# The blockwise recurrence of a decoder layer: 16x16 inverses by halves, two DMA queues, new issue times

## The chip, the cores and the metric

The kernel runs on one core of one Trainium2 chip, as one launch. The metric is the device time of an execution in microseconds; the median of several runs is compared. The engines are TensorE (PE: matrix products and transposes), VectorE (DVE), ScalarE (ACT), GpSimd (Pool) and SyncE (SP, which here only issues transfers).

## The reference

One layer of a decoder on 256 tokens of width 1024, float32. Two token mixers run side by side on the normalised input and come from one combined input projection: an RWKV-7 recurrence of 8 heads of 64, and softmax attention of 8 heads of 64. Both are projected, gated, summed and projected again; a gated MLP with a width-3 convolution follows. The part that matters here is the recurrence, one state of 64x64 for each head:

```python
def step(state, inp):
    r_t, w_t, k_t, v_t, a_t, b_t = inp           # a_t = -kk, b_t = kk * a
    sa = jnp.einsum('bhvk,bhk->bhv', state, a_t)
    state = (state * w_t[:, :, None, :] + sa[..., None] * b_t[:, :, None, :]
             + v_t[..., None] * k_t[:, :, None, :])
    return state, jnp.einsum('bhvk,bhk->bhv', state, r_t)
...
x = x + (g_a * u_a + g_b * u_b) @ w_out[l]
x = x + conv_ffn(rms_norm(x, norm2_g[l]), w_ffn_up[l], ffn_conv_w[l], ffn_conv_b[l], w_ffn_down[l])
```

## The kernel before, in words

All large products are done with a number split in two parts. Weights arrive from memory as `raw` tiles of 512 KB, loaded by SP into 4 buffers. ACT rounds each to a high half (`whi`, L259), DVE subtracts to get the low half (`wlo`, L269, 3 buffers), and PE uses both. One weight tile feeds two bulk blocks of PE, each of 12 matmuls with 256 columns (L302, L304, L307) or 6 with 512 columns (L323, L324, L327).

The recurrence is computed in 4 chunks of 64 tokens for 8 heads. Within a chunk it needs the inverse of a unit triangular 64x64 matrix for each of 32 pairs of head and chunk. In order of the program:

- `KB` (L645, L647) are keys scaled by the decay, one product of them on Pool; `AR` (L651) holds the other factors. PE turns KB (`pk`, L670; ACT copies to `KBt`, L673).
- PE multiplies KB and AR into `pgr` (L682) in two halves of 32 matmuls; DVE masks them into `G` (L686). Both halves use the same four PSUM banks.
- The diagonal 16x16 blocks of G go out to memory (`d1`, L707) and back as `Tb` (L709), one block on each of 128 partitions. DVE inverts them row by row, 15 steps of a product and a sum (L717, L719), copies the transpose (L720), and SP writes both forms, `Xb`, to memory (`d2`, L722). 24 transfers bring them back into `X` (L729), 16 on SP and 8 on Pool. X[:, 0] holds the inverse, X[:, 1] its transpose.
- PE turns the values (`pv`, L748) and multiplies them by G (`pz`, L760). Then come the bonus and gate products (`ch`, `pg`, L841 to L846), which take one weight tile of their own; Pool casts a part of it (L833) for L846.
- PE joins the 16-blocks to 32 and then 64: `pp` (L791, reads X[:, 0]), DVE masks it to `P` (L797), `px` (L808, L818, read X[:, 1]), DVE adds into X (L801, L824, L827), and once more.
- Four chunk steps follow (L933 to L973), each with a group normalisation (L892 to L903, with one operation on Pool, L900), whose result PE turns (`pc`, L910).

The order of PE's work is written out by hand. The recurrence (`chain`), the attention (`att`), the normalisation (`gn`) and the bulk projections (`bulk`) are generators. Each yields a cost and a latency; a planner keeps a clock, adds the cost to it, and calls a generator again once the clock has passed the time of its last yield plus its latency. The bulk generator has latency 0 and fills what is left. A bulk block costs 0.33 x 4 or 0.65 x 2. A number `yield 0, 11.0` is thus an issue time: bulk work of 11 in the plan is put ahead of what follows. PE executes in the order of issue. On the other engines and queues the framework's scheduler sets the order. `taken` counts the weight tiles, and `GATE_AT` is the place of the gate tile in the queue of loads; the assertion at L831 ties it to the plan.

After the generators come the second branch projection, the output projection and the MLP, which the change does not touch.

Of the kernel before, what the change touches and what calls it, by code (L numbers as in the profile page):

```python
# [9 lines left out]
F32 = mybir.dt.float32  # L10
# [3 lines left out]
OP = mybir.AluOpType  # L14
AX = mybir.AxisListType
# [13 lines left out]
HALF = 8  # L29
NORM_EPS = 1e-6  # L30
GN_EPS = 64e-5
GATE_AT = 30
SLACK = {"chain": 1.7, "att": 1.4, "lv1": 2.5, "gn": 2.0}
DEC = math.exp(-0.5)
NEG = -3.0e38
# [2 lines left out]
def body(tc, x, positions, norm1_g, w_in, rwkv_mu, w_decay_up, decay_bias, w_aaa_up,  # L38
         aaa_bias, w_gate_up, k_k, k_a, r_k, ln_g, ln_b, q_norm_g, k_norm_g, w_branch_a,
         w_branch_b, w_out, norm2_g, w_up, conv_w, conv_b, w_down, out):  # L40
    nc = tc.nc
    act, dve, pool, pe = nc.scalar, nc.vector, nc.gpsimd, nc.tensor
    ctx = ExitStack()
    with ctx:
# [22 lines left out]
        def b2(name, shape, dt=F32):  # L67
            return sb.tile(shape, dt, name=name, tag="b2", bufs=9)
# [95 lines left out]
            return par[:, i:i + 1]  # L164

        wdu = cst.tile([128, CW], F32, name="wdu")
        cst.tile([128, 848], F32, name="gap")
        gqk = cst.tile([128, 2, 64], F32, name="gqk")
        posi = sb.tile([128, 2], I32, name="posi")

# [1 line left out]
        for r, n in ((mu1[0:1792].rearrange("(n c) -> n c", c=128), 14),  # L172
# [3 lines left out]
            dst = p1[at_:at_ + n]  # L176
# [341 lines left out]
        def ch16(t):  # L518
            return t.rearrange("p a (c i) -> p (a c) i", i=64)
# [31 lines left out]
        def need(nm, d):  # L551
            while nm not in d:
                yield 0, 0.5
# [6 lines left out]
        def chain():  # L560
# [71 lines left out]
            def kbv(q, a):  # L632
                return KB[:, 64 * q:64 * q + 2048].rearrange("p (u a i) -> p u a i", a=2, i=64)[:, :, a]
# [8 lines left out]
            bb = av  # L642
            dve.tensor_tensor(flat(bb), flat(kk), flat(av), op=OP.mult)
            yield 0, 1.0
            pool.tensor_tensor(kbv(0, 1), ch16(bb), ch16(e3), op=OP.mult)  # L645
            for q, hs in PAR:
                dve.tensor_tensor(kbv(q, q)[hs], ch16(kp)[hs], ch16(e3)[hs], op=OP.mult)  # L647
                yield 0, 1.0
# [7 lines left out]
            G = [b8(f"G{q}", [128, 16, 128]) for q in range(2)]  # L656
            d1 = dr.tile([128, 256], F32, name="d1")
            d2 = dr.tile([8, 2, 16, 256], F32, name="d2")
            Tb = sb.tile([128, 16, 16], F32, name="Tb")
            def banks(nm):  # L660
                return [[(chp if j else atp)(nm) for _ in range(2)] for j in range(2)]

            yield 0, 4.0

            KBt = [b2("KBt", [128, 4, 128]) for _ in range(3)]
            pk = [[p.rearrange("p (c a i) -> p c a i", c=2, a=4) for p in pj] for pj in banks("pk")]
# [4 lines left out]
            for c in range(3):  # L671
                for q, hs in PAR:
                    act.copy(KBt[c][:, :, hs], pk[c // 2][q][:, c % 2])  # L673
            yield 1.4, 4.0
            masks()
            for g in range(2):
                pg = [[p.rearrange("p (u i) -> p u i", u=4) for p in pj] for pj in banks("pgr")]
                for ct in (2 * g, 2 * g + 1):
                    for c in range(4):
                        u = 4 * ct + c  # L680
                        for q, hs in PAR:
                            pe.matmul(pg[ct % 2][q][:, c], kb(q, u), AR[hs, u].rearrange("p a i -> p (a i)"),  # L682
                                      start=True, stop=True)
                for ct in (2 * g, 2 * g + 1):
                    for q in range(2):
                        last_g = dve.tensor_tensor(G[q][:, gslot(ct):gslot(ct) + 4], pg[ct % 2][q],  # L686
                                                   gmask[:, None, :].to_broadcast([128, 4, 128]), op=OP.mult).ins
                yield 2.1, (5.0, 0.1)[g]
            bp = zr
            bph, bpl = by("bph", dt=F32R), by("bpl", dt=F32R)  # L690
            xgh, xgl = b2("xgh", [128, 2, S], F32R), t1("xgl", dt=F32R)
# [11 lines left out]
            for q, hs in PAR:  # L703
                for b in range(4):
                    q0 = bsl(q).start + 16 * b
                    r0 = (q * 4 + b) * 16
                    nc.sync.dma_start(d1[r0:r0 + 16].rearrange("u (j i) -> j u i", j=16),  # L707
                                      G[q][q0:q0 + 16, :, 16 * b:16 * b + 16])
                nc.sync.dma_start(Tb[hs], d1[hs].rearrange("u (j i) -> u j i", j=16))  # L709
            Xb = b2("Xb", [128, 2, 16, 16])  # L710
            dve.memset(Xb[:, 0], 0.0)
            dve.memset(Xb[:, 0].rearrange("p i n -> p (i n)")[:, 0:256:17], 1.0)
            tmp = sb.tile([128, 64], F32, name="tmp")
            for j in range(15):
                ni, nn = 15 - j, j + 1
                tv = tmp[:, :ni * nn].rearrange("p (i n) -> p i n", i=ni)
                dve.tensor_tensor(tv, Tb[:, j, j + 1:16][:, :, None].to_broadcast([128, ni, nn]),  # L717
                                  Xb[:, 0, j, 0:nn][:, None, :].to_broadcast([128, ni, nn]), op=OP.mult)
                dve.tensor_tensor(Xb[:, 0, j + 1:16, 0:nn], Xb[:, 0, j + 1:16, 0:nn], tv, op=OP.add)  # L719
            dve.tensor_copy(Xb[:, 1], Xb[:, 0].rearrange("p i n -> p n i"))  # L720
            for xx in range(2):
                nc.sync.dma_start(d2[:, xx], Xb[:, xx].rearrange("p i n -> p (i n)"))  # L722
            X = b8("X", [128, 2, 16, 64])
            pool.memset(X, 0.0)

            def to_x(eng, side, x, us_, src):
                b = src[1]
                q0 = bsl(side).start + 16 * b
                eng.dma_start(X[q0:q0 + 16, x, us_, 16 * b:16 * b + 16],  # L729
                              d2[4 * src[0] + b, x, src[2]].rearrange("u (i n) -> i u n", i=16))  # L730

            for q in range(2):
                for b in range(4):
                    to_x(nc.sync, q, 0, slice(0, 16), (q, b, slice(0, 16)))
            for q in range(2):
                for b in range(4):
                    for a in range(2):
# [1 line left out]


            yield from need("v", zs)
            zv = zs["v"]
            VU = b8("VU", [128, 4, 2, 4, 64])
            pv = [chp("pv").rearrange("p (j a n) -> p j a n", j=2, a=4) for _ in range(2)]
# [81 lines left out]
                    v = level(1, w, X[bsl(a), 1, 8 * q + 1:8 * q + 8:2])  # L826
                    dve.tensor_tensor(v, v, p[1][bsl(1 - a), 0:4], op=OP.add)  # L827

            yield 0, 11.0
            yield 0, 2.0  # L830
            assert taken[0] == GATE_AT, taken[0]  # L831
            wgh, wgl = weights()
            pool.tensor_copy(wgh[64:128, 1], wgl[64:128, 1].bitcast(F32))  # L833
# [542 lines left out]
```

## Time and profile before

| | us |
|---|---|
| median of 3 runs | 405.56 |
| lowest and highest | 405.13, 407.06 |
| span of the profiled execution, first to last instruction | 403.9 |
| PE busy | 396.4 |
| DVE busy | 324.6 |
| ACT busy | 233.9 |
| Pool busy | 41.8 |

The page tells of one profiled execution. It gives the span from its first to its last instruction, and not that execution's own device time; the three runs lie 1.2 to 3.2 above the span. "Idle before" is the time in which an engine did nothing, with the instruction or transfer whose end let it go on. A wait that ended with "issue" has no releaser in the profile. A line of the timeline has the start, the duration, the engine, the line of the program, the operation and out<-in; "x" counts the instructions merged. Times in the text are in us from the start of the span.

### The profile page before, as it was taken

The numbers are of one execution on the slowest core, as the hardware profiler recorded it, in microseconds if no ns is written. First come the engines' busy times: TensorE is split into PE (matmuls) and PEld (weight loads), VectorE is DVE, ScalarE is ACT, GpSimd is POOL, SyncE is SP. The second block draws the span as 40 slices with busy tenths as digits, with TensorE's granted clock in tenths as the row PEclk, the third lists the DMA queues.
The fourth block names the chain that finished last, engine by engine and source line by source line (L and its number), as shares of the span: only waits on it lengthen the run. The fifth ranks groups of instructions, "written<-read, shape, count | busy, mean of one in ns | idle before, by whom it ended". The sixth has DMA issues, their size and how long they took to land.

```text
span 403.9 us, 8280 instructions
## 1 busy us (share of the span) xinstructions
PE 396.4 (98%) x3250; PEld 348.7 (86%) x3250; DVE 324.6 (80%) x574; ACT 233.9 (58%) x397; POOL 41.8 (10%) x69
## 2 busy tenths in 40 slices
PE   7999999999989999999999999999999999999996
PEld 3999989788989989999888888888888888888885
DVE  3988999899667978778965898977869778687694
ACT  6799755475647676444563784655546446355440
POOL 7910070010500011020011000000000000000000
PEclk9999999999999999999999999999999999999999
DMA  8954555564783444536563756676665665656612
GB/s 243 317 168 154 160 161 158 160 176 150 159 220 104 115 150 131 183 112 207 191 183 97 242 157 208 181 232 189 200 204 163 208 187 177 207 174 209 196 48 104
DMA packets 61990, 70.53 MB, mean 175 GB/s; under 512 B 9421, under 2 KB 52243, under 8 KB 61952
## 3 DMA queue, kind: packets, MB, share of 16 engines
q1 hardware_dynamic: 61104, 69.54, 57.1%
q0 software_dynamic: 832, 0.47, 0.6%
q8 instruction: 25, 0.41, 0.5%
q14 instruction: 13, 0.11, 0.1%
q10 hardware_dynamic: 16, 0.00, 0.0%
HBM read 68.56 MB, written 1.44 MB: 173 GB/s over the span
## 4 chain that ended last, share of the span: by engine, by line
PE 93%; DVE 2%; ACT 1%; DMA 1%; issue 1%; SPq 0%; POOL 0%; DVEq 0%; POOLq 0%; ACTq 0%
PE acc L1262 15%; PE acc L302 9%; PE acc L304 8%; PE acc L307 8%; PE acc L1267 8%; PE at L1262 5%; PE acc L323 5%; PE acc L327 5%; PE acc L324 5%; PE f L1286 5%; PE f L1282 5%; PE f L1284 4%; PE at L1267 3%; PE acc L461 1%; DMA x<-in_x_dram 1%; PE pgr L682 1%
## 5 line engine op out<-in xcount | busy, mean ns | idle before, releaser
L259 ACT CAST whi<-raw 128x1024 fp32r<-128x1024 f32 x120 | 125.7, 1051 | 106.0 <-PE acc L1262 22.2
L269 DVE TENSOR_TENSOR wlo<-raw,whi 128x1024 fp32r<-128x1024 f32 x121 | 148.8, 1234 | 26.2 <-PE acc L1267 12.2
L1262 PE MATMUL acc<-hx,whi 128*128 128x512 f32 x264 | 68.2, 393 | 0.0
L302 PE MATMUL acc<-hx,whi 128*128 128x256 f32 x232 | 58.3, 287 | 0.0
L304 PE MATMUL acc<-hx,whi 128*128 128x256 f32 x232 | 55.9, 277 | 0.0
L1262 PEld LDWEIGHTS acc<-hx,whi 128*128 128x128 f32 x264 | 47.0, 188 | 8.1
L302 PEld LDWEIGHTS acc<-hx,whi 128*128 128x128 f32 x232 | 43.6, 188 | 2.0 <-issue 0.8
L304 PEld LDWEIGHTS acc<-hx,whi 128*128 128x128 f32 x232 | 43.6, 188 | 0.1
L1267 PEld LDWEIGHTS acc<-h,wlo 128*128 128x128 f32 x264 | 37.1, 188 | 3.6
L1267 PE MATMUL acc<-h,wlo 128*128 128x256 f32 x264 | 37.8, 279 | 0.0
L307 PE MATMUL acc<-hx,wlo 128*128 128x256 f32 x232 | 35.7, 277 | 0.0
L1284 PE MATMUL f<-whi,hb 128*128 128x512 f32 x80 | 31.2, 390 | 0.0
L1286 PE MATMUL f<-wlo,hb 128*128 128x512 f32 x80 | 31.2, 390 | 0.0
L1282 PE MATMUL f<-whi,hb 128*128 128x512 f32 x80 | 31.2, 389 | 0.0
L307 PEld LDWEIGHTS acc<-hx,wlo 128*128 128x128 f32 x232 | 30.6, 188 | 0.0
L1262 PE MATMUL at<-hx,whi 128*128 128x512 f32 x88 | 24.0, 392 | 0.0
L1272 DVE TENSOR_REDUCE an<-acc 128x256 f32<-128x512 f32 x22 | 14.2, 685 | 9.3 <-PE acc L1267 9.3
L1262 PEld LDWEIGHTS at<-hx,whi 128*128 128x128 f32 x88 | 16.4, 188 | 3.6
L323 PE MATMUL acc<-whi,hx 128*128 128x512 f32 x48 | 19.1, 399 | 0.0
L324 PE MATMUL acc<-whi,hx 128*128 128x512 f32 x48 | 18.8, 391 | 0.0
L1286 PEld LDWEIGHTS f<-wlo,hb 128*128 128x128 f32 x80 | 15.0, 188 | 3.2
L1284 PEld LDWEIGHTS f<-whi,hb 128*128 128x128 f32 x80 | 15.0, 188 | 2.8
(331 smaller groups left out, 688.5 us busy)
## 6 DMA issues: line engine op xcount, KB each, us to landing
raw<-in_w_ffn_up_dram SPq DMA_DIRECT2D x44, 512.0 KB, 4.3
raw<-in_w_in_dram SPq DMA_DIRECT2D x37, 512.0 KB, 4.3
raw<-in_w_ffn_down_dram SPq DMA_DIRECT2D x22, 512.0 KB, 4.0
raw<-in_w_out_dram SPq DMA_DIRECT2D x8, 512.0 KB, 4.1
x<-in_x_dram SPq DMA_DIRECT2D x8, 256.0 KB, 4.4
early<-in_w_in_dram SPq DMA_DIRECT2D x4, 512.0 KB, 7.6
raw<-in_w_branch_b_dram SPq DMA_DIRECT2D x4, 512.0 KB, 3.4
raw<-in_w_branch_a_dram SPq DMA_DIRECT2D x4, 512.0 KB, 3.5
```

The costliest lines, as they stand in the source:

```text
L259: act.copy(wide(hi, k, c), spread(raw, k, c))
L269: eng.tensor_tensor(wide(lo, k, c), spread(raw, k, c), wide(hi, k, c).bitcast(F32), op=OP.subtract)
L302: pe.matmul(om, wh[:, k, ms], xh[:, k0 + k], start=k0 + k + m == 0, stop=False, skip_group_check=True)
L304: pe.matmul(om, wh[:, k, ms], xl[:, k0 + k], start=False, stop=False, skip_group_check=True)
L307: pe.matmul(om, wl[:, k, ms], xh[:, k0 + k], start=False, stop=k0 + k == nk - 1 and m == n - 1, skip_group_check=True)
L323: pe.matmul(ps_[t], xh[:, K, ts], wh[:, k], start=K == 0, stop=False)
L324: pe.matmul(ps_[t], xl[:, K, ts], wh[:, k], start=False, stop=False)
L1262: pe.matmul(ps_[m], wh[:, k, m * 128:m * 128 + 128], hx[:, k0 + k].rearrange("p a s -> p (a s)"), start=k0 + k == 0, stop=False, skip_grou ...
L1267: pe.matmul(ps_[m][:, 0:S], wl[:, k, m * 128:m * 128 + 128], h2[k0 // 4][:, k], start=False, stop=k0 + k == 7, skip_group_check=True)
L1282: pe.matmul(fin[f], hb[:, 0, i, ts], wh[:, 0, cs], start=st, stop=False, skip_group_check=f == 3)
L1284: pe.matmul(fin[f], hb[:, 1, i, ts], wh[:, 0, cs], start=False, stop=False, skip_group_check=f == 3)
L1286: pe.matmul(fin[f], hb[:, 0, i, ts], wl[:, 0, cs], start=False, stop=False, skip_group_check=f == 3)
```

## The change

Five edits, all in the recurrence:

1. The Pool product of KB (L645) goes to DVE.
2. The 16x16 blocks are inverted by halves: the four 4x4 blocks on the diagonal row by row (4 small operations), then 4 to 8 and 8 to 16, each as two products with `product`: all terms into `tmp`, then a reduction. Tb is read back in the order in which it was written, one contiguous row for each partition, and DVE transposes while it copies into Xb. The two memsets of Xb become one of the diagonal. Tb and Xb are 272 wide, so that the diagonal blocks can be addressed with one stride.
3. The transfers of d1, Tb, d2 and the first 8 of X alternate between SP and Pool, by side. The queues then have 4 + 1 + 1 + 12 each, where SP had 8 + 2 + 2 + 16 and Pool 8.
4. Issue times: ahead of pk 4.0 becomes 2.0, behind pk 4.0 becomes 3.5, between the two pgr 5.0 becomes 3.0, ahead of pv 1.5 is new, and ahead of the gate products 11.0 + 2.0 becomes 6.0. GATE_AT follows, 30 to 27.
5. Places in memory: `gap`, a tile that nothing uses, shrinks from 848 to 336 columns, `tmp` moves to the shared buffers `b2`, Xb gets a place of its own, and `wv` is new.

```diff
-GATE_AT = 30
+GATE_AT = 27
...
-        cst.tile([128, 848], F32, name="gap")
+        cst.tile([128, 336], F32, name="gap")
...
-            pool.tensor_tensor(kbv(0, 1), ch16(bb), ch16(e3), op=OP.mult)
+            dve.tensor_tensor(kbv(0, 1), ch16(bb), ch16(e3), op=OP.mult)
...
-            Tb = sb.tile([128, 16, 16], F32, name="Tb")
+            Tb = sb.tile([128, 272], F32, name="Tb")
...
-            yield 0, 4.0
+            yield 0, 2.0
...
-            yield 1.4, 4.0
+            yield 1.4, 3.5
...
-                yield 2.1, (5.0, 0.1)[g]
+                yield 2.1, (3.0, 0.1)[g]
...
-                    nc.sync.dma_start(d1[r0:r0 + 16].rearrange("u (j i) -> j u i", j=16),
-                                      G[q][q0:q0 + 16, :, 16 * b:16 * b + 16])
-                nc.sync.dma_start(Tb[hs], d1[hs].rearrange("u (j i) -> u j i", j=16))
-            Xb = b2("Xb", [128, 2, 16, 16])
-            dve.memset(Xb[:, 0], 0.0)
-            dve.memset(Xb[:, 0].rearrange("p i n -> p (i n)")[:, 0:256:17], 1.0)
-            tmp = sb.tile([128, 64], F32, name="tmp")
-            for j in range(15):
-                ni, nn = 15 - j, j + 1
-                tv = tmp[:, :ni * nn].rearrange("p (i n) -> p i n", i=ni)
-                dve.tensor_tensor(tv, Tb[:, j, j + 1:16][:, :, None].to_broadcast([128, ni, nn]),
-                                  Xb[:, 0, j, 0:nn][:, None, :].to_broadcast([128, ni, nn]), op=OP.mult)
-                dve.tensor_tensor(Xb[:, 0, j + 1:16, 0:nn], Xb[:, 0, j + 1:16, 0:nn], tv, op=OP.add)
-            dve.tensor_copy(Xb[:, 1], Xb[:, 0].rearrange("p i n -> p n i"))
+                    (nc.sync, nc.gpsimd)[q].dma_start(d1[r0:r0 + 16].rearrange("u (j i) -> j u i", j=16),
+                                                      G[q][q0:q0 + 16, :, 16 * b:16 * b + 16])
+                (nc.sync, nc.gpsimd)[q].dma_start(Tb[hs, 0:256], d1[hs])
+            Xb = sb.tile([128, 2, 272], F32, name="Xb")
+            tmp = b2("tmp", [128, 512])
...
+            X0 = Xb[:, 0]
+            dve.tensor_copy(X0[:, 0:256].rearrange("p (i n) -> p i n", n=16),
+                            Tb[:, 0:256].rearrange("p (j i) -> p i j", i=16))
+            dve.memset(X0[:, 0:256:17], 1.0)
+            td, xd = diagonal(Tb), diagonal(X0)
+            for j in (1, 2):
+                ni = 3 - j
+                tv = tmp[:, 0:4 * ni * j].rearrange("p (b i n) -> p b i n", b=4, i=ni)
+                dve.tensor_tensor(tv, td[:, :, j, j + 1:4][:, :, :, None].to_broadcast([128, 4, ni, j]),
+                                  xd[:, :, j, 0:j][:, :, None, :].to_broadcast([128, 4, ni, j]), op=OP.mult)
+                dve.tensor_tensor(xd[:, :, j + 1:4, 0:j], xd[:, :, j + 1:4, 0:j], tv, op=OP.add)
...
+            def product(dst, x, y, n):
+                tv = tmp[:, 0:n * n * n].rearrange("p (i m k) -> p i m k", i=n, m=n)
+                dve.tensor_tensor(tv, x[:, :, None, :].to_broadcast([128, n, n, n]),
+                                  y.rearrange("p k m -> p m k")[:, None, :, :].to_broadcast([128, n, n, n]),
+                                  op=OP.mult)
+                dve.tensor_reduce(dst, tv, axis=AX.X, op=OP.add)
+            for n in (4, 8):
+                for o in range(0, 16, 2 * n):
+                    w = wv[:, 0:n * n].rearrange("p (i m) -> p i m", i=n)
+                    product(w, square(Tb, o, o + n, n).rearrange("p k i -> p i k"), square(X0, o, o, n), n)
+                    product(square(X0, o + n, o, n), square(X0, o + n, o + n, n), w, n)
+            dve.tensor_copy(Xb[:, 1, 0:256].rearrange("p (n i) -> p n i", n=16),
+                            X0[:, 0:256].rearrange("p (i n) -> p n i", i=16))
             for xx in range(2):
-                nc.sync.dma_start(d2[:, xx], Xb[:, xx].rearrange("p i n -> p (i n)"))
+                (nc.sync, nc.gpsimd)[xx].dma_start(d2[:, xx], Xb[:, xx, 0:256])
...
-                    to_x(nc.sync, q, 0, slice(0, 16), (q, b, slice(0, 16)))
+                    to_x((nc.sync, nc.gpsimd)[q], q, 0, slice(0, 16), (q, b, slice(0, 16)))
...
             yield from need("v", zs)
+            yield 0, 1.5
...
-            yield 0, 11.0
-            yield 0, 2.0
+            yield 0, 6.0
```

More of the change, by code (lines that the diff above doesn't have):

```diff
@@ new lines, in chain, with square, diagonal @@
+                (nc.sync, nc.gpsimd)[q].dma_start(Tb[hs, 0:256], d1[hs])
+            Xb = sb.tile([128, 2, 272], F32, name="Xb")
+            tmp = b2("tmp", [128, 512])
+            def square(t, r0, c0, n):
+                return t[:, 16 * r0 + c0:16 * r0 + c0 + 16 * n].rearrange("p (i n) -> p i n", n=16)[:, :, 0:n]
+            def diagonal(t):
+                return t[:, 0:272].rearrange("p (b r) -> p b r", r=68)[:, :, 0:64].rearrange(
+                    "p b (i n) -> p b i n", n=16)[:, :, :, 0:4]
@@ new lines, in chain @@
+            wv = sb.tile([128, 64], F32, name="wv")
+            def product(dst, x, y, n):
[9 more added lines that the diff above has]
+                    product(square(X0, o + n, o, n), square(X0, o + n, o + n, n), w, n)
```

## The prediction

> **What bounds the kernel now.** I read the page's head first, then who TensorE (PE) waits for, then the busy time by stage, and only then the rows of the changed stage.
>
> ```profile
> span 403.9 us, 8280 instructions
> PE 396.4 (98%) x3250; PEld 348.7 (86%) x3250; DVE 324.6 (80%) x574; ACT 233.9 (58%) x397; POOL 41.8 (10%) x69
> ```
>
> The list of PE's waits (who waited for whom: us in total, times, longest):
>
> ```profile
> PE idle L109 <- DVE eps L374: 1.5, 1, 1.5
> PE px L808 <- issue: 1.1, 1, 1.1
> PE pc L910 <- DVE yc L903: 0.6, 1, 0.6
> PE xt L414 <- DVE xn L408: 0.6, 1, 0.6
> ```
>
> Busy time by stage (stretch, its length, then PE, PEld, DVE, ACT, POOL, granted clock, DMA share, GB/s):
>
> ```profile
> 14.00:60.00 46.00, 46.00 (x407) 42.90 (x406) 42.68 (x68) 35.48 (x58) 14.65 (x24) 1.00 0.61 184
> 60.00:110.00 50.00, 50.00 (x453) 44.30 (x453) 44.26 (x108) 30.42 (x50) 6.53 (x11) 1.00 0.60 162
> 110.00:184.00 74.00, 72.22 (x1152) 67.20 (x1151) 57.74 (x118) 43.74 (x103) 6.48 (x9) 1.00 0.50 146
> ```
>
> PE is busy in 98% of the span. The list of PE's waits is complete: two belong to the start, which the change does not touch, and two to the recurrence, 1.1 and 0.6. The stretches 14 to 60 and 60 to 110, where the vector engine (DVE) runs at 93% and 89%, cost PE nothing: it is busy for 46.00 of 46.00 and 50.00 of 50.00. The granted clock is 1.00 throughout. The change removes no matmul, so what it can win is about the 1.7 us of recurrence waits; what it can lose has no such ceiling.
>
> **The change part by part.** PE runs in the order in which the planner hands out work, so shorter issue times only reorder PE. A bulk block costs 1.32 or 1.30 in the plan (0.33 x 4, 0.65 x 2) and 1.36 on PE, the distance of the first two rows here; the second fence has the recurrence's stages (start us, us, then the instruction).
>
> ```profile
> 64.20 0.28 PE L302 MATMUL acc<-hx,whi 128*128 128x256 f32 x1
> 65.56 0.28 PE L302 MATMUL acc<-hx,whi 128*128 128x256 f32 x1
> ```
>
> ```profile
> 60.48 0.97 PE L670 MATMUL pk<-ident,KB 64*128 64x64 f32 x24
> 67.02 2.06 PE L682 MATMUL pgr<-AR,KB 64*128 64x128 f32 x32
> 74.70 2.06 PE L682 MATMUL pgr<-AR,KB 64*128 64x128 f32 x32
> 84.62 1.16 PE L760 MATMUL pz<-VU,G 64*64 64x64 f32 x64
> 105.60 0.28 PE L846 MATMUL pg<-xgh,whi 128*128 128x256 f32 x1
> 114.93 1.14 PE L791 MATMUL pp<-X,G 64*64 64x32 f32 x64
> 118.83 0.82 PE L808 MATMUL px<-P,X 64*64 64x32 f32 x41
> 120.70 0.49 PE L808 MATMUL px<-P,X 64*64 64x32 f32 x20 [1.05 <-issue]
> 146.94 0.41 PE L910 MATMUL pc<-ident,yc 128*128 128x128 f32 x2 [0.63 <-DVE yc L903]
> ```
>
> Stepping the planner through both sets of yields gives the bulk blocks between stages. Between the key product and pk there are 2 fewer blocks; between pk and the first pgr 3 instead of 4 (3.5 / 1.32 rounds up to 3, 4.0 to 4), between the two pgr 3 instead of 4, between the second pgr and pz 8 instead of 5 (the new 1.5 and where it falls), and from pz to the gate product 8 instead of 14. So pk moves to 60.48 - 2 x 1.36 = 57.8, pgr to 62.9 and 69.3, pz to 83.3, the first L846 to 105.60 - 7 x 1.37 = 96.0. That is three weight tiles less, which agrees with GATE_AT 27 for 30. Then pp comes at 105.4 and px at 109.5: the attention's two transposes of 0.65 that stood before pp now come behind it, and 5 blocks stand where 4 stood. No block is added or lost. What remains is whether each input is there.
>
> Pool's product. These rows price it:
>
> ```profile
> 51.26 1.22 DVE L643 TENSOR_TENSOR av<-sq,av 128x1024 f32<-128x1024 f32 x1
> 56.49 2.74 DVE L269 TENSOR_TENSOR wlo<-raw,whi 128x1024 fp32r<-128x1024 f32 x1
> 52.65 5.50 POOL L645 TENSOR_TENSOR KB<-av,L 128x1024 f32<-128x1024 f32 x1 [30.96 <-DVE av L643]
> ```
>
> It takes 5.50 us on Pool and ends at 58.15; the same shape takes DVE 1.22, so KB would be ready at about 53.7, 4 us ahead of pk at 57.8. On Pool it would be 0.35 late. DVE gains 1.22 of work in a stretch where it is 93% busy. Against that, one weight split (L269) took 2.74 during the Pool product where its like takes 1.22: 1.52 may come back. Net DVE cost between -0.3 and +1.2; I take 0 for PE, because PE never waited for a split in this stretch. [...]
>
> The earlier G. pgr's second half needs the banks that the first half's mask products free. The nearest rows are DVE's:
>
> ```profile
> 68.78 2.47 DVE L686 TENSOR_TENSOR G<-pgr,gmask 128x512 f32<-128x512 f32 x4
> ```
>
> and, for the inversion, the groups of DVE between 60 and 110 (count, busy us, mean ns):
>
> ```profile
> L719 DVE TENSOR_TENSOR Xb<-Xb,tmp 128x15 f32<-128x15 f32 (+7 forms) x15 | 3.1, 204 | 0.3
> L717 DVE TENSOR_TENSOR tmp<-Tb,Xb 128x15 f32<-128x15 f32 (+7 forms) x15 | 3.0, 202 | 0.3
> L994 DVE TENSOR_REDUCE r<-s 128x8 f32<-128x512 f32 x2 | 1.3, 659 | 0.4 <-ACT s L992 0.4
> L848 DVE TENSOR_TENSOR zr<-ch,zv 128x512 f32<-128x512 f32 x1 | 0.7, 684 | 0.0
> L720 DVE COPY Xb<-Xb 128x256 f32<-128x256 f32 x1 | 0.4, 390 | 0.0
> ```
>
> pgr's first half would end at 64.9. If DVE takes the mask products then, the first two banks are free by 66.2 and PE at 69.3 waits for nothing; if they start no earlier than now, at 68.78, plus 1.22 of added work, the first two end at 71.2 and PE waits 2.0. I take 0.3, near the low end, because the splits that stood ahead of these products belong to tiles that PE now needs later.
>
> The inversion. Before: 3.0 + 3.1 + 0.4 and two memsets of 0.35 together, about 6.9 us in 33 dependent instructions. After: two copies at 0.39, a memset under 0.1, four small products at 0.16, four products and four reductions of 64 at 0.203 (the mean of the old steps, which have 15 to 64 elements), two products of 512 at 0.684 and two reductions of 512 at 0.659: 0.78 + 0.07 + 0.64 + 1.62 + 1.37 + 1.32 = 5.8 us in 19 instructions. The reductions of 64 have no row; between 0.16 and 0.66 each the total lies between 5.6 and 7.6. This saves PE nothing by itself: nobody on PE waits for it.
>
> The transfers, by the rows of SP and Pool, and then the times to landing (in order: G to memory, Tb, X from SP, X from Pool):
>
> ```profile
> 85.31 0.46 SPq L709 DMA_DIRECT2D Tb<-d  x1
> 101.88 1.39 SPq L722 DMA_DIRECT2D d<-Xb  x2
> 105.22 7.62 SPq L729 DMA_DIRECT2D X<-d  x16
> 112.95 6.69 SPq L236 DMA_DIRECT2D raw<-in_w_in_dram  x5
> 103.55 1.47 POOL L833 CAST whi<-wlo 64x512 fp32r<-64x512 f32 x1 [15.41 <-DVE wlo L269]
> 107.01 4.30 POOL L729 DMA_DIRECT2D X<-d  x8 [1.98 <-DMA d<-Xb]
> ```
>
> ```profile
> DMA to landing us min/median/max: 1.6/1.7/2.0
> DMA to landing us min/median/max: 4.6/4.6/4.6
> DMA to landing us min/median/max: 1.8/1.9/2.7
> DMA to landing us min/median/max: 1.9/2.1/2.4
> ```
>
> One issue costs about 0.47 on SP and 0.53 on Pool. With G ready at 72.7 (1.7 behind the second pgr's end, as now), four issues, 1.7 to land, one Tb issue and 2 to 4.6 to land, Tb is there at 79 to 81.5. It was issued at 85.31 and took 4.6 in the queue with weight loads; Pool's half avoids that queue. The inversion then ends at 87 to 92, Xb lands 2 to 3 later, and each queue issues 12 transfers of X (SP 5.6 us, Pool 6.4): the last X lands between 98 and 103.5. pp needs its half at 105.4, px the rest at 109.5, so both are covered by at least 2 us. If Tb comes later than DVE's order expects, the weight splits behind the inversion wait with it; three wlo buffers of 2.7 us of PE each are the cover.
>
> [...] The unused tile "gap" shrinks by 512 columns to make room for the wider Xb; I price it at 0, since no row ties time to placement.
>
> The two waits. The 1.05 at px stands between instructions of one kind and waits for nothing that the profile shows. It falls where five 512 KB loads, held back behind SP's 16 X issues until 112.95, are in flight. After the change SP is held 5.6 rather than 7.6 us, and px comes at 109.5, about 9 behind the end of SP's X issues rather than 6. Bounds: it goes (-1.05), or stays or moves elsewhere (0), or appears twice (+1.05). I take -1.05, because the queue ahead of it drains earlier. [...] At pc the group normalisation has 6.5 us of other PE work ahead of it instead of 6.1, so 0.63 becomes about 0.3; bounds 0 and 1.2.
>
> Sum: -1.05 - 0.3 + 0.3 = -1.05 us, so a span of 402.8. The profiled execution's time outside its span is not on the page; the median of the runs, 405.56, stands 1.7 above the span, and I carry that over: 404.5.
>
> **The rivals.**
> (1) Nothing moves: the pause at px is bound to the density of small matmuls and comes back, pc as before: 405.6. For it: the same 96 small matmuls follow each other in px. Against it: the other dense stages, pp and pgr, show no such pause.
> (2) Slower, by Pool's queue. L833 casts half of the gate weights on Pool, takes 1.47 and ended at 105.02, 0.6 before the first L846. It now has to end by 96.0. If the 12 X issues (from 91, when Xb has landed, for 6.4 us) stand ahead of it in Pool's order, it ends at 91 + 6.4 + 1.5 = 98.9 and PE waits 2.9 at L846, with all bulk work behind it: 405.56 - 1.05 + 2.9 = 407.4, up to 409 if Xb lands 2 later. It decides as soon as Xb lands before the gate tile's low half is split. Now Xb landed at 107.0, behind the cast; by my working the two come within 2 us of each other.
> (3) All recurrence waits go and nothing new comes: 405.56 - 1.7 = 403.9. A busy PE is not PE at its peak, so the true waits can be longer than listed; I allow 0.7 for that, down to 403.2.
> (4) The vector engine holds pgr back by 2.0: 405.56 - 1.35 + 2.0 = 406.2.
>
> **How the numbers follow.** Chances: forecast 0.45 (its own range 403.6 to 405.2), rival 1 0.18, rival 2 0.20, rival 3 0.12, rival 4 0.05. Half a per cent, 2.0 us, is about what a measurement of this kernel can tell from no change. Faster than 403.5 takes rival 3 and the edge of the forecast: 0.15. Slower than 407.6 takes the upper half of rival 2 and what I have not thought of: 0.18. Same: 0.67. The range takes in all cases but the tails, with 0.2 below rival 3 for the spread of the runs: 403.0 to 408.2.
>
> **What would show it.** Right: KB written by DVE before 55, pk near 57.8, pgr near 62.9 and 69.3, the gate product near 95.4, the last X landed before 104, a list of PE's waits without px. Rival 2: PE's wait at pg L846 with Pool as releaser. Rival 4: a wait at pgr L682. Wrong altogether: a wait of PE for weight splits (L269) around the inversion, a Tb that lands after 84, or a PE busy time that differs by more than the waits.

## The result and the profile after

The changed kernel takes 411.67 us (median of 6 runs, 411.05 to 413.25); the kernel before took 406.33 beside it. The ratio is 1.0121, with a 95% interval of [1.0091, 1.0152]: slower by 1.2%, where 404.5 was forecast. The profiled execution of the changed kernel took 413.25, the longest of its runs, with a span of 411.2.

The head of the page of the changed kernel, the list of PE's waits (in total, times, longest) and the busy time by stage follow, in the order in which the prediction shows them of the kernel before:

```profile
span 411.2 us, 8270 instructions
PE 399.6 (97%) x3250; PEld 350.0 (85%) x3250; DVE 328.0 (80%) x561; ACT 233.2 (57%) x397; POOL 42.7 (10%) x78
```

```profile
PE xt L414 <- DVE xn L408: 1.5, 1, 1.5
PE idle L109 <- DVE eps L374: 1.5, 1, 1.5
PE acc L323 <- DVE qkv L1027: 1.2, 1, 1.2
PE pS L986 <- DVE yf L945: 0.8, 1, 0.8
PE pc L940 <- DVE yc L933: 0.7, 1, 0.7
PE acc L327 <- DVE wlo L269: 0.6, 1, 0.6
PE acc L302 <- ACT whi L259: 0.6, 1, 0.6
PE pv L779 <- DVE zv L491: 0.5, 1, 0.5
PE acc L461 <- DVE hx L422: 0.4, 1, 0.4
```

```profile
14.00:60.00 46.00, 45.37 (x388) 41.67 (x389) 42.30 (x66) 35.33 (x56) 11.08 (x22) 1.00 0.54 163
60.00:110.00 50.00, 47.64 (x421) 41.45 (x421) 46.40 (x100) 27.34 (x48) 12.63 (x23) 1.00 0.59 162
110.00:184.00 74.00, 72.44 (x1154) 66.77 (x1153) 55.08 (x112) 44.04 (x105) 5.17 (x6) 1.00 0.49 145
```

Two waits on the list belong to the start (L414, L461) and are longer here than in the execution shown of before; in the profiles of the variants below they come and go (first row of the table), so that part is the profiled execution's. The pause at px is gone. Five waits are new: L302 in the stretch 14 to 60, pv, L327 and L323 between 60 and 110, and pS (L986) in the chunk steps. All but L302 have the vector engine as releaser. The stretch 60 to 110, in which PE had been busy for 50.00 of 50.00, now has 47.64.

The listed waits understate it. I therefore took, for every matmul, the distance to the next start beyond the median distance for its shape in the kernel before, and summed that by stage. A stage begins with the first matmul that it names; pss (L603) is the norm of the keys. The table has the differences to the kernel before, in us, each from the one profiled execution; its columns are the changed kernel and six variants that the experiments introduce. The sums agree with the differences of the spans within 0.3:

| stage | after | memset_held | place_only | after_old_times | times_only | inv_later | late_t12 |
|---|---|---|---|---|---|---|---|
| first 14 us | +1.3 | +0.3 | 0.0 | -0.4 | -0.6 | +0.3 | -0.4 |
| 14 to pss (L603) | +1.8 | -0.1 | 0.0 | +1.4 | +0.1 | 0.0 | -0.1 |
| pss to pv | +0.1 | 0.0 | 0.0 | +0.1 | +0.6 | +0.2 | 0.0 |
| pv to the gate product | +3.1 | +3.1 | +2.2 | +6.9 | +1.5 | +0.6 | +0.9 |
| gate product to pp | 0.0 | 0.0 | 0.0 | +0.1 | +3.1 | +1.1 | -0.1 |
| pp to the last pc | +0.3 | +0.3 | -0.2 | -1.6 | +2.9 | +9.4 | +1.7 |
| behind it | +0.6 | +0.6 | 0.0 | 0.0 | +0.6 | +0.6 | -0.3 |
| sum | +7.2 | +4.2 | +2.0 | +6.6 | +8.2 | +12.2 | +1.8 |

Apart from the start, the loss of the changed kernel thus has two main places, 14 to pss and pv to the gate product. The experiments ask why.

### The profile page after: what moved, and what is told of

Its sections match the earlier page's. It is cut to its first block, busy times and chain, and to the rows that moved or that the text cites. A ratio compares the mean times of both kernels' runs of the same rounds, so it can differ in the third digit from the quotient of the medians.

```text
span 411.2 us, 8270 instructions
## 1 busy us (share of the span) xinstructions
PE 399.6 (97%) x3250; PEld 350.0 (85%) x3250; DVE 328.0 (80%) x561; ACT 233.2 (57%) x397; POOL 42.7 (10%) x78
## 4 chain that ended last, share of the span: by engine, by line
PE 77%; DVE 12%; ACT 4%; issue 2%; DMA 2%; POOL 2%; SPq 0%; DVEq 0%; POOLq 0%; ACTq 0%
PE acc L1292 15%; PE acc L1297 7%; PE acc L302 6%; PE acc L307 5%; PE acc L304 5%; PE at L1292 5%; PE f L1314 4%; PE f L1316 4%; PE f L1312 4%; PE acc L323 3%; PE acc L327 3%; PE acc L324 3%; DVE wlo L269 3%; PE at L1297 2%; POOL X L759 1%
## 5 line engine op out<-in xcount | busy, mean ns | idle before, releaser
L302 PE MATMUL acc<-hx,whi 128*128 128x256 f32 x232 | 59.0, 289 | 0.6 <-ACT whi L259 0.6
L302 PEld LDWEIGHTS acc<-hx,whi 128*128 128x128 f32 x232 | 43.6, 188 | 3.1 <-issue 0.8
L323 PE MATMUL acc<-whi,hx 128*128 128x512 f32 x48 | 19.2, 401 | 1.2 <-DVE qkv L1027 1.2
```

What stands on the lines that cost most here:

```text
L302: pe.matmul(om, wh[:, k, ms], xh[:, k0 + k], start=k0 + k + m == 0, stop=False, skip_group_check=True)
L323: pe.matmul(ps_[t], xh[:, K, ts], wh[:, k], start=K == 0, stop=False)
```

## The experiments

### First: which part loses

The first four take the change apart. Theories: T, the issue times; P, the places in memory; I, the new inversion as load on the vector engine.

**times_only**, the kernel before with the new issue times:

```diff
-GATE_AT = 30 ; yield 0, 4.0 ; yield 1.4, 4.0 ; (5.0, 0.1)[g] ; yield 0, 11.0 and 0, 2.0
+GATE_AT = 27 ; yield 0, 2.0 ; yield 1.4, 3.5 ; (3.0, 0.1)[g] ; yield 0, 1.5 (pv) ; yield 0, 6.0
```

> The kernel before with the six new issue times alone; inversion row by row, one queue, KB product on Pool. Theory T (the new issue times bunch DVE's work: query/key norms, inversion and weight splits fall together): slower than before by 3 to 9 us, as the old inversion also brings X later than pp wants it; PE waits at L323/L327 and at pp. Theory P (the new places in memory slow the kernel from its first microseconds): the same as before within 1 us apart from a wait at pp. Theory I (the new inversion is what loads DVE): no more than a wait at pp for X.

Measured: 414.51, ratio 1.0181 [1.0147, 1.0216]. The issue times alone cost more than the whole change. PE waits 1.4 at L846 for Pool's cast, which itself starts late, at 97.77, after 6.60 of waiting for the vector engine, and not behind transfers of X (Pool issues these from 105.53 on). It waits 0.8 at pS, 0.7 at pc and 0.5 at pv. And pp runs in two pieces of 32 matmuls, at 110.40 and 112.69, each as long (1.12) as all 64 together in the kernel before (1.14). There they start four at a time, here two at a time, with a bulk block between the pieces: the scheduler has changed the order on PE. That it did so because X comes late is likely, but no run shows it.

**after_old_times**, the changed kernel with the old issue times (the same diff, reversed):

> The changed kernel with the old issue times. Theory T: back to the time of before, 405 to 407 us, no wait of PE at L323/L327 near 97. Theory P: still 3 us slower than before, with 24.5 instead of 22.9 us at the end of the first ident product and 42 instead of 39 at pss. Theory I: still 2 to 3 us slower, with waits for weight splits around the inversion.

Measured: 412.68, ratio 1.0158 [1.0125, 1.019]. Theory T as the sole cause falls: without the new times the change is no faster. PE now waits 3.1 at L323, but the waits at pv and pS are gone.

**place_only**, the kernel before with the new places:

```diff
-cst.tile([128, 848], F32, name="gap")
+cst.tile([128, 336], F32, name="gap")
-Tb = sb.tile([128, 16, 16], ...)    Xb = b2("Xb", ...)      tmp = sb.tile([128, 64], ...)
+Tb = sb.tile([128, 272], ...)       Xb = sb.tile([128, 2, 272], ...)   tmp = b2("tmp", [128, 512])
```

> The kernel before with the new places alone: gap 336 columns, Tb and Xb 272 wide and Xb and wv of their own, tmp in a b2 buffer; every operation as before. Theory P: slower by about 3 us, lost before 42 us. Theories T and I: the same as before, within 0.3%; then the 3 us that the changed kernel's profile lost before 42 us are spread from run to run.

Measured: 408.65, ratio 1.0068 [1.004, 1.0096]. I had priced this at 0. The first 85 us are those of the kernel before, so the mechanism that theory P named is wrong; the loss is one wait of PE, and the vector engine's rows show where it comes from (timeline: start, us, then the instruction and what ended its idle time):

```profile
PE acc L323 <- DVE Xb L720: 1.7, 1, 1.7
```

```profile
90.20 0.18 DVE L718 TENSOR_TENSOR tmp<-Tb,Xb 128x15 f32<-128x15 f32 x1 [4.16 <-DMA Tb<-d]
91.57 0.68 DVE L995 TENSOR_REDUCE r<-s 128x8 f32<-128x512 f32 x1
93.18 0.69 DVE L998 TENSOR_TENSOR qkv<-acc,r 128x512 f32<-128x512 f32 x1
```

In the kernel before (there L994 is the norm's first operation and L717 the inversion's first product):

```profile
85.08 0.69 DVE L994 TENSOR_REDUCE r<-s 128x8 f32<-128x512 f32 x1 [0.40 <-ACT s L992]
90.55 0.16 DVE L717 TENSOR_TENSOR tmp<-Tb,Xb 128x15 f32<-128x15 f32 x1
```

The vector engine stands idle for 4.16 us with the first product on Tb at its head, while the attention's norms, which were ahead of it in the kernel before, wait behind. The norms read PE's accumulators (L998, which ends at 93.87), so the accumulators come free late and PE waits at L323 until 94.01. The profile names a step of the inversion (L720) as what ended the wait, because that step ended last, at 93.97. Nothing of the inversion's work has changed here: only its place in the vector engine's order.

**inv_only**, the kernel before with the new inversion and its places, one queue and the old times:

> The kernel before with the inversion by halves alone (and the places that it needs): old issue times, transfers on one queue as before, KB product on Pool. Theory I: slower by 1 to 3 us, with PE waits for weight splits at 90 to 105. Theory T: the same as before within 0.3%. Theory P: slower by 3 us, as the placement.

Measured: 409.9, ratio 1.0078 [1.0049, 1.0108], with a wait of 3.3 at L323. Its interval overlaps that of place_only, so by time the two can't be told apart. Theory I as a load is not needed for the wait; its being 1.6 longer than in place_only leaves room for some of it.

### Second: the early fill of X

In the changed kernel the vector engine has two small operations near 25 us that last as long as a fill of X on Pool, and in the kernel before it has neither (timeline of the changed kernel, then of the kernel before):

```profile
24.78 1.87 DVE L194 CAST posf<-posi 128x2 f32<-128x2 int32 x1
24.85 1.83 DVE L148 TENSOR_SCALAR m<-m,rowf 128x64 f32<-128x64 f32 x1
24.37 2.26 POOL L754 MEMSET X<- 128x2048 f32 x1 [1.21 <-issue]
```

```profile
23.15 0.15 DVE L194 CAST posf<-posi 128x2 f32<-128x2 int32 x1
23.22 0.24 DVE L148 TENSOR_SCALAR m<-m,rowf 128x64 f32<-128x64 f32 x1
58.08 1.82 POOL L724 MEMSET X<- 128x2048 f32 x1
```

As long as the product of KB was on Pool, the fill stood behind it and ran at 58. With the product gone nothing holds the fill, and it moves up by 34 us. L194 starts at 24.78 and ends at 26.65, L148 at 26.68, and the fill at 26.63: the two end within 0.05 us of it. The fill in turn takes 2.26 instead of 1.82, 0.44 more, and a cast of the vector engine that had begun before it (L261, 24.18 to 24.86) ends 0.49 behind its start. Theory M reads these rows so: the early fill holds up L194 and L148, and PE is late by it (below, this hold-up is called the lock). What causes it, no run shows.

**kb_dve_only**, the kernel before with the product on DVE and nothing else:

```diff
-pool.tensor_tensor(kbv(0, 1), ch16(bb), ch16(e3), op=OP.mult)
+dve.tensor_tensor(kbv(0, 1), ch16(bb), ch16(e3), op=OP.mult)
```

> The kernel before with one edit: the product of KB (L645) on the vector engine instead of Pool. Places, issue times, inversion and queues are as before. [...] Rival theory K (the product of KB is a win where it stands and the loss of the first 42 us has another cause, for instance the later loads of the profiled run): L194 and L148 as before, pss at 39.2, the time 405 to 406.

**kb_held**, the same with the fill held behind KB:

```diff
-pool.memset(X, 0.0)
+tiny = sb.tile([128, 1], F32, name="tiny")
+held = pool.tensor_copy(tiny, KB[:, 64:65])
+with tc.issue_after(held.ins):
+    pool.memset(X, 0.0)
```

> As kb_dve_only, but a copy of one column of KB on Pool is put ahead of the fill of X, and the fill is ordered behind it, so that it starts at about 54 to 58 us as in the kernel before. Theory M: L194 and L148 back at 0.15 and 0.24, pss at 39.2, the time that of before, 405.5 to 406.5; the difference to kb_dve_only is the price of the lock alone, 1.4 us. Theory K: no difference to kb_dve_only.

Measured: kb_dve_only 407.32, ratio 1.0043 [1.0027, 1.006]; kb_held 405.92, ratio 0.9995 [0.9978, 1.0011]. The difference is 1.40 us, the price of the lock. L194 and L148 take 1.86 and 1.82 in kb_dve_only and end at 24.90 and 24.93, the fill there at 24.87; in kb_held they take 0.16 and 0.25. The first bulk product and pss, in kb_dve_only and then in kb_held:

```profile
9.67 2.39 PE L461 MATMUL acc<-hx,whi 128*128 128x256 f32 x16
40.49 1.20 PE L603 MATMUL pss<-bones,sq 64*64 64x1 f32 x64
```

```profile
10.36 2.39 PE L461 MATMUL acc<-hx,whi 128*128 128x256 f32 x16
39.72 1.12 PE L603 MATMUL pss<-bones,sq 64*64 64x1 f32 x64
```

The distance is 30.82 in the one and 29.36 in the other: 1.46 us, and theory M is shown. The rival K falls: the product on the vector engine wins nothing by itself. The delay reaches PE by way of ACT, whose head waits for the vector engine's scan (L579), so that a weight cast comes late (kb_dve_only):

```profile
29.06 1.06 ACT L581 ACTIVATE sg<-L 128x1024 f32<-128x1024 f32 x1 [1.55 <-DVE L L579]
32.91 0.38 PE L302 MATMUL acc<-hx,whi 128*128 128x256 f32 x1 [0.59 <-ACT whi L259]
```

**memset_held**, the changed kernel with the same edit:

> The changed kernel with the same copy and order on Pool, so that the fill of X starts behind KB. Theory M: stretch 24 to 40 us takes PE 18.5 us of work again instead of 19.9, the time is 1.4 us below the changed kernel, 410.2; the rest of the loss stays. Rival theory O (the whole loss is the order on the vector engine around the inversion): no difference to the changed kernel, 411.7.

Measured: 410.73, ratio 1.0116 [1.0097, 1.0135], 0.94 below the changed kernel. L194 and L148 are back at 0.16 and 0.24, and the row "14 to pss" of the table is at -0.1, where the changed kernel has +1.8. The 0.94 alone would not be clear of noise, since the two ratios' intervals overlap; with the row and with kb_held, some 1 to 1.4 of 5.3 us is explained. The wait at L323 is unmoved.

### Third: the inversion ahead of the norms

**place_late** takes place_only and moves the inversion, unchanged, in the program behind pz, so that the norms come first:

```diff
 yield 1.4, 3.0          (behind pz)
+Xb = ... ; the 15 steps ; d2 ; X and its transfers     (moved here)
```

> The kernel before with the new places only (as in place_only, row-by-row inversion, one queue, old issue times), and the inversion moved in the program behind pz. Theory O (the places cost time only because the inversion then comes ahead of the norms on the vector engine and its head waits for Tb): the wait at L323 of 1.7 goes and the time is that of the kernel before, 405.5 to 406.5. Theory P (the places themselves cost): 408.6 as place_only.

Measured: 406.15, ratio 0.9998 [0.9976, 1.0021]. The wait at L323 is gone and with it the whole loss of place_only, with gap, Tb, Xb and tmp of the same sizes and kinds (X and VU, which take their buffers in the order of the program, change places by the move). So these places cost nothing by themselves; what they changed is the order that the scheduler chose for the vector engine. Why it chose another one, no run shows.

The changed kernel has the same order, though there Tb is in time (timeline of its vector engine):

```profile
84.23 0.38 DVE L723 COPY Xb<-Tb 128x256 f32<-128x256 f32 x1
88.34 0.68 DVE L1024 TENSOR_REDUCE r<-s 128x8 f32<-128x512 f32 x1
94.91 0.68 DVE L1024 TENSOR_REDUCE r<-s 128x8 f32<-128x512 f32 x1
95.78 1.21 DVE L269 TENSOR_TENSOR wlo<-raw,whi 128x1024 fp32r<-128x1024 f32 x1
97.03 1.17 DVE L269 TENSOR_TENSOR wlo<-raw,whi 128x1024 fp32r<-128x1024 f32 x1
98.11 0.68 DVE L1027 TENSOR_TENSOR qkv<-acc,r 128x512 f32<-128x512 f32 x1
```

The inversion runs from 84.23 to 94.6 and the first norm is woven into it; the second starts at 94.91. No weight split ends between 87.4 and 97.0 (PE's wait at L327), and the accumulator that PE wants at L323 is read at 98.11.

**inv_later**, the changed kernel with the same move:

> The changed kernel with the block that inverts, from the fill of the diagonal to the transfers of X, moved in the program behind pz and its yield. The attention's second normalisation then stands ahead of the inversion in the vector engine's order, the fill of X comes behind Pool's Tb transfer at about 75 us, and the cast at L833 (L863 in the changed kernel) ahead of Pool's X transfers. Theory O (the inversion ahead of the norms keeps the accumulators occupied and the weight splits away, so that PE waits 1.8 us and more at L327 and L323 from 96 to 99): those waits go, and with the fill out of the way too the time is 3.5 to 4 us below the changed kernel, 407.7 to 408.2; the last X lands later, 104 to 108, and a wait of up to 2 us may come at pp or px. Theory M alone: 410.2, as memset_held. Theory T (what is left is the new issue times): no more than 1.4 us gained in both kernels.

Measured: 417.79, ratio 1.0287 [1.0264, 1.031], 6 us worse than the changed kernel where 3.5 to 4 less was expected. In the table the stage from pv to the gate product falls from +3.1 to +0.6, so theory O (the order on the vector engine is the loss) holds there. But the inversion now ends at 103.6 and X comes late:

```profile
117.08 1.16 PE L839 MATMUL px<-P,X 64*64 64x32 f32 x17 [2.71 <-DMA X<-d]
```

and the stage from pp to the last pc loses 9.4 us and not 2.7. The busy time of PE by stretches (stretch, length, busy, granted clock, DMA share, GB/s) shows the larger part of why:

```profile
114.00:117.00 3.00, 0.36 (x2) 0.84 1.10 355
117.00:120.00 3.00, 2.92 (x63) 0.50 0.76 245
120.00:126.00 6.00, 6.00 (x44) 0.50 0.02 5
126.00:128.00 2.00, 2.00 (x100) 0.94 0.00 0
```

By these rows the clock is at half from about 116.0 to 126.2 (twice the missing clock, ahead of 117 and behind 126), and PE works from 117.1 on: some 9.2 us at half the clock, which by my estimate costs 4.6. Of the rest, PE waits 0.4 at pp and 0.8 at pS; what is left was not taken apart. I come back to the clock in the last section.

**after_sp_queue**, the changed kernel with one queue as before:

```diff
-(nc.sync, nc.gpsimd)[q].dma_start(...)     (d1, Tb, d2, the first 8 of X)
+nc.sync.dma_start(...)
```

> The changed kernel with all these transfers on one queue (X: 16 on SyncE and 8 on Pool, as before). Theory O: the vector engine's head waits for Tb until 88 to 90, the norms stand behind it, PE waits 3 us or more at L323 and the clock halves behind that wait, X lands 4 us later against an early pp: 414 to 418. Rival theory N (the second queue does nothing for PE): 411.7 as the changed kernel.

Measured: 416.26, ratio 1.0256 [1.0227, 1.0284]. The vector engine's head waits for Tb until 88.22 and PE waits 4.0 at L327. The second queue is thus worth 4.6 us inside the changed kernel; with it Tb is there when the new order asks for it (no wait in front of L723).

**queues_only**, the kernel before with two queues (the same diff, reversed, in the kernel before):

> The kernel before with the transfers of G, Tb, Xb and X divided over two queues and nothing else changed. Here too the scheduler puts the inversion ahead of the norms on the vector engine. Theory O: if Tb lands at 81 to 84 through two queues (in the changed kernel it did not hold the vector engine up), the norms and splits behind it are late by the 6.9 us of the row-by-row inversion less what interleaves, PE waits 1 to 2 us at L323 around 95, 407 to 409. Theory Q (two queues help: X earlier, the pause at px gone): 404.5 to 405.5.

Measured: 411.95, ratio 1.0152 [1.0122, 1.0183], 3 us above what theory O gave. PE's longest wait is the one that I had made rival 2 of the prediction:

```profile
PE pg L846 <- POOL whi L833: 2.8, 1, 2.8
```

Pool's cast stands behind 12 transfers of X, ends at 112.20 instead of 105.0, and PE waits 2.8 (2.9 was the price in the prediction). Behind the wait the clock is at half for 3.4 us.

### Fourth: is it those two alone?

**late_old**, the changed kernel with the fill held, the norms first and the old issue times:

> The changed kernel with the old issue times, the fill of X held behind KB, and the inversion moved in the program behind pz, so that the attention's norms stand first on the vector engine. KB on the vector engine, the inversion by halves and the two queues stay. Theory O (the order on the vector engine and the fill of X are what the change loses, and the old issue times leave X enough time): no wait at L323 or L327, X landed by 112 for a pp at 115 and a px at 119, the clock undisturbed, and the time that of the kernel before or up to 1 us less if the pause at px goes: 405 to 406.3. Theory T (the parts that stay have a price of their own): 407.5 or more. Rival: X lands after 119 as it did at 117 with the new issue times, PE waits at px, the clock halves behind the wait, 409 or more.

Measured: 414.54, ratio 1.021 [1.0175, 1.0245], a miss by 8 us. The expected waits are gone, and there is one that no theory named, on ScalarE (PE's wait, then ACT's timeline):

```profile
PE ps L1076 <- ACT qkT L1058: 7.0, 1, 7.0
```

```profile
119.67 1.04 ACT L259 CAST whi<-raw 128x1024 fp32r<-128x1024 f32 x1 [6.67 <-DMA raw<-in_w_in_dram]
121.14 1.04 ACT L259 CAST whi<-raw 128x1024 fp32r<-128x1024 f32 x1 [0.43 <-DMA raw<-in_w_in_dram]
122.09 1.07 ACT L1058 COPY qkT<-pqk 128x512 f32<-128x512 f32 x2
```

In the changed kernel SP issues the next weight load only behind its share of X (at 102.63, X from 96.63 on); I take it to be so here too. ACT's head waits 6.67 for a load, and the copies of the attention's keys, which are ready, stand behind the casts. In the kernel before they stood ahead of them.

**late_pp** and **late_t12** are inv_later with more time for X:

```diff
-yield 0, 2.8      (ahead of pp)          late_pp:  +yield 0, 6.8
-yield 0, 6.0      (ahead of the gate)    late_t12: +yield 0, 12.0 ; GATE_AT = 29
```

> inv_later with one issue time changed: 6.8 instead of 2.8 ahead of pp, three bulk blocks or about 4 us more between the gate product and pp. In inv_later X was late for px by 2.7 us and the clock halved for 10 us behind that. Theory O (fill of X and order on the vector engine are the loss): PE's waits at pp and px go, with them the half clock, and the stage from pp to the chunk steps loses 9 us less: 407 to 409; of the loss against before, the wait at the gate product of 1.0 and the waits of the chunk steps of 0.8 are left. Theory T (the new issue times cost of their own): 410.5 to 412. Rival A: three weight casts now stand ahead of the score copies on ScalarE, and PE waits at the scores as in late_old: 412 or more.

> inv_later with the issue time ahead of the gate product 12.0 instead of 6.0 (the gate tile in place 29 instead of 27). Theory O: X is in time for pp and px, no half clock, and the wait at the gate product goes too: 406 to 408. Theory T: 410 or more with waits in the chunk steps. Rival A: a head-of-queue wait at another place, behind weight casts on ScalarE: 409 or more.

Measured: late_pp 409.54, ratio 1.0099 [1.0065, 1.0134]; late_t12 408.07, ratio 1.0061 [1.004, 1.0082]. late_t12 is 3.6 us faster than the changed kernel, with the inversion's place in the program moved and one issue time partly taken back; late_pp's interval overlaps that of the changed kernel. late_pp missed its 407 to 409: X is in time, but PE waits 1.0 at the gate product, 1.0 at pc and 0.5 at pb, and the clock is halved for 3.4 us behind the last two. In late_t12 1.8 us are left. Its largest waits are 0.5 at pv, 1.1 at pc and 0.8 at a chunk step, all of them for the vector engine at stages that the new issue times reach earlier or with less bulk work ahead, and a pause of 0.6 at px that waits for nothing the profile shows. No version here is faster than the kernel before; kb_held and place_late equal it.

## Why the prediction was wrong, step by step

- **What bounds the kernel, and the list of waits.** Right, also in that the gain had a ceiling of 1.7 us and the loss none. But I then priced the losses one by one, by durations, and none by its place in an engine's order.
- **PE's order.** Right for the stages. memset_held, whose fill does not meet L194 and L148, has pk at 58.01, the two pgr at 63.2 and 69.5; forecast were 57.8, 62.9 and 69.3. late_pp, where nothing waits at L323, has its first L846 (L876 there) at 96.5; 96.0 was forecast. Within a stage the scheduler changes PE's order too, other than the description of the kernel says: in the changed kernel a bulk block stands between L875 at 102.3 and L876 at 104.29, which are neighbours in the program.
- **Pool's product.** The duration was right (1.22 on the vector engine), KB was ready at 57.9, or 54.8 without the 3.1 by which everything ran late there (pss at 42.25 instead of 39.16), instead of 53.7, and PE did not wait for it. The price of 0 failed: I named what the vector engine would gain or lose at 53, and did not ask what Pool would do in the freed time. Behind the product stood the fill of X, and without the product it ran at 24. It costs 1.4 us (kb_dve_only against kb_held). Nor is 5.50 us Pool's own pace, as I took it: in the profile of the kernel before, the vector engine's operations with two inputs run at their usual 1.2 us from 50.14 to 55.80, then comes a reduction, and only the split that starts at 56.49 takes 2.74 and ends behind Pool's product. The five other profiles with the product on Pool have the same order (5.48 to 5.50, and 2.58 to 2.76). It looks as if Pool waited first and the vector engine then; by that reading the product itself takes some 2.3 us (55.8 to 58.15), an estimate that no run isolates.
- **The earlier G.** No wait at pgr; 0.3 was near enough, and rival 4 did not come.
- **The inversion.** It takes 7.3 us by its rows against my 5.8. That this lies under my upper bound of 7.6 is luck: the bound allowed for slow reductions of 64, and these took 0.21 to 0.22. The products of 512 took 1.07 and 1.18 where I took 0.684 from a row with plain operands, those of 64 took 0.27 instead of 0.203, and the last copy 0.68 instead of 0.39. The copy took 0.68 in just the three kernels where a fill of P on Pool begins beside it (the changed one, memset_held and after_sp_queue) and 0.37 to 0.39 in all others. In the changed kernel the copy runs from 93.91 to 94.59 and the fill from 93.92 to 94.44; L194 was longer beside a fill too. "This saves PE nothing by itself: nobody on PE waits for it" was the step that failed. PE waits for what stands behind it. I had the sign on my list ("the weight splits behind the inversion wait with it") but tied it to a late Tb and gave it no price; the order does it with Tb in time, for 2.2 to 2.5 of the 3.1 us between pv and the gate product (+0.9 in late_t12, +0.6 in inv_later).
- **The places.** "I price it at 0, since no row ties time to placement" was right as to these places and wrong as to the edit: it came with another order, at 0.7% (place_only against place_late).
- **The transfers.** Tb landed at 83.4, or 80.3 without the same 3.1; forecast were 79 to 81.5. (The sum there is 0.4 short: 69.3 + 2.06 + 1.7 gives G at 73.1 and not 72.7.) The last X landed at 107.3 (104.2), just behind my 98 to 103.5, and pp at 112.0 was covered. The second copy of Xb ends at 94.59, ahead of Pool's first issue that needs it at 94.89, and Pool's issues of X took 0.53 to 0.58 each, against a price of 0.53.
- **The pauses.** px's went, as forecast, but the reason that I gave (an earlier end of the loads behind X) no run tests, and late_t12, with the same two queues, has a pause of 0.6 at px: this part of the sum may be luck. pc's did not shrink: 0.7 instead of 0.3.
- **Rival 2** had the order right: the cast stood behind 12 issues of X and ended at 104.2. PE lost 0.1 by it, since it was itself late by 3 and had a bulk block ahead of L876. In queues_only the wait came, at 2.8. In times_only PE waited 1.4 at the same place, but by another way: there the cast stood ahead of X and its own input was late.
- **New issue times.** I counted blocks and asked whether the recurrence's inputs are there. I did not ask it of pv (0.5) and of the chunk steps (0.8 at pS, which stands behind the same normalisation as pc). Both waits are there in times_only, 0.5 and 0.8, and neither is in after_old_times, so they belong to the issue times.

So of 5.3 us, 0.9 to 1.4 is the early fill (measured), about 2.2 to 2.5 the inversion ahead of the norms (shown by place_only and place_late in the kernel before, and by one stage of inv_later and late_t12 in the changed one), and the rest, some 1.5 to 2, what the new issue times lose at pv, at the gate product and in the chunk steps less the pause at px; late_t12 stands 1.85 above the kernel before with the first two gone. This last share is read from the waits and was not taken apart further.

## What to carry to other kernels

When an operation is taken off a queue, look at what stood behind it: it will run earlier, and there it may hold up something that was in the clear (1.4 us here). Where a scheduler sets the order on an engine, a local edit can change that order, and the price of the edit is that of the work which then stands behind a wait, so compare the order of every engine before pricing durations. On a kernel whose bound engine is busy for 98%, a reordering can gain about the sum of that engine's waits (1.7 here), and a single new wait can cost more than that (3.1 in after_old_times).

## What the hardware showed that I had not expected

A pause of PE can cost more than its length. After the 3.1 us at L323, PE runs at half the clock in after_old_times (columns as in inv_later):

```profile
95.00:98.00 3.00, 0.10 (x1) 1.00 0.00 0
98.00:99.00 1.00, 1.00 (x4) 0.86 0.46 125
99.00:102.00 3.00, 3.00 (x8) 0.50 0.75 156
102.00:103.00 1.00, 1.00 (x5) 0.94 0.52 57
```

Twice the missing clock gives the time at half speed: 0.28 + 3.0 + 0.12 = 3.4 us. The same sum gives 3.4 in inv_only, times_only, queues_only and late_pp, 6.8 in after_sp_queue and late_old, and 10.2 in inv_later: one, two or three times 3.4. Why they come in this length, no run shows. In after_old_times PE has 8 matmuls in the 3.00 us from 99 to 102, where the kernel before has 15 in as long (95 to 98, at a clock of 1.00); by that I estimate that 3.4 us cost 1.7 where PE is busy throughout.

In each of these eight profiles PE was busy for little more than half of the 3.4 us just ahead of the half clock, or less: 0.00 us in late_old, 0.52 in inv_only, 0.53 in after_sp_queue, 0.81 in after_old_times, 1.35 in queues_only, 1.75 in inv_later, 1.92 in late_pp and 1.96 in times_only. The changed kernel has such a stretch too (1.73 from 96.54 to 99.94) and kept a clock of 1.00 in the profiled execution, so the busy time just ahead does not decide it alone; what else does, no run shows. Nor does it take one long gap: the halving in times_only followed waits of 0.4 and 1.4 that ended 3 us apart.

The five profiled executions with 3.4 us at half the clock have a mean granted clock of 0.994 to 0.996, and that of the changed kernel, with none, has 1.0. By that mean I take some executions of a kernel to have such a stretch and others not. With one wait of 1.7 (place_only), 6 of 12 executions had a mean granted clock below 0.997; those took 408.5 to 411.7, and the others 407.4 to 408.8. With waits of 3.1 and more (after_old_times, inv_only, late_old) it was 17 of 18; in the changed kernel, with 0.6 and 1.2, 1 of 6; and in the kernel before, beside the experiments, 10 of 69.
